# Split weights of the up stages at a place of their own in every group of 16 blocks (a two-layer decoder trunk on one core)

## The chip, the cores and the metric

The program runs on one core of a Trainium2 chip, in one launch. The metric is the time of one execution in microseconds (us) on the device. TensorE (PE) multiplies: a matmul loads up to 128 columns of weights (PEld in the profile) and then moves the columns of the other operand past them. VectorE (DVE), ScalarE (ACT) and GpSimd (POOL) do the elementwise work, and SyncE (SP) issues the large transfers. All of them work on a memory of 128 partitions (SBUF); the place of a tile is a byte address, the same in every partition.

## The reference

256 tokens of width 1024 pass two layers. Layer 0 has a mixer of two attention groups, layer 1 a latent attention; each is followed by the same channel mixer over 16384 single-neuron experts, and a norm ends the trunk. Of the channel mixer this matters here:

```python
def peer_ffn(h, w_q, sub_keys, u_tab, v_tab):
    ...
        q = (xc @ w_q).reshape(t, PEER_HEADS, 2, PEER_QDIM // 2)
        sc = jnp.einsum('thpc,hpnc->thpn', q, sub_keys).astype(jnp.float32)
        v_half, i_half = lax.top_k(sc, PEER_TOPK_HALF)
        ...
        top_s, pos = lax.top_k(cand, PEER_TOPK)
        expert = jnp.take_along_axis(cand_idx, pos, axis=-1)
        g = jax.nn.softmax(top_s, axis=-1)
        u = u_tab[expert]
        act = jax.nn.gelu(jnp.einsum('thkd,td->thk', u, xc).astype(jnp.float32), approximate=False)
        w = (g * act).astype(xc.dtype)
        return jnp.einsum('thk,thkd->td', w, v_tab[expert])
```

`u_tab` and `v_tab` are 16384 x 1024 in float32.

## The kernel before

The kernel gathers no experts. It multiplies the tokens with all of `u_tab` (the **up stage**), applies the gate, which is zero for experts that were not chosen, and multiplies with all of `v_tab` (the **down stage**). Both tables are cut into 128 blocks of 128 experts. A block of `u_tab` arrives as one `raw` tile of 128 x 1024, eight pieces of 128 x 128 side by side, one for each eighth of the model's width.

To keep float32's precision, every weight is split into two parts: `hi`, a copy by ACT into the type float32r (line 69), and `lo`, what is left, subtracted by DVE (line 70). The class `Weights` does this in halves of 512 columns. Its list `units` has an access pattern and a width for every `raw` tile in the order of use. `split` takes a `hi` tile from the pool `hip` and a `lo` tile from `lop`, with five buffers of 128 x 512 each, and runs four halves ahead of the use; `load` fetches `raw` two units ahead. Weights of all stages pass through this class.

In the up stage the split weights are the loaded operand, and the tokens' tiles `hi[c]` and `lo[c]` (128 x 256, eight of each, made once a layer) move past them. `split_prod` (line 814) multiplies one half: four pieces by three products, `hi` with `hi` (line 819), `hi` with the tokens' `lo` (line 820), and `lo` with `hi` (line 821). So a block has 24 matmuls of 128 x 128 weights and 256 moving columns into one tile `S`, and a layer has 3072. Between the halves `bg.pump` puts in pieces of background work: the routing on DVE, and from about block 33 on the gates, whose 512 small matmuls a layer stand on line 1011. In the down stage and in the projections the roles are exchanged: there the split weights move, 512, 352 or 200 columns at a time (lines 1099 to 1101 and 301 to 303).

Pools take their places one after the other: `cp` (tokens `x`, the identity matrix `ident` and other constants), `rawp`, `hip`, `lop`, `small`, then a tile `fill` of 192 bytes that nothing uses, and behind it the pools of the stage. As the program is built, `x`, `ident`, `raw`, all buffers of `hip` and `lop`, and the stages' tiles for the tokens' parts and the gates begin 160 bytes past a multiple of 512. The work tiles `rr` of the first mixer begin at a multiple of 512, and `ks` of the second one at 416 past one. The 200-column projection takes two 200-column pieces from one half, 800 bytes apart. A transpose (lines 288, 497 and 713) loads the tile that it turns and moves `ident` past it.

Of the kernel before, what the change touches and what calls it, by code (L numbers as in the profile page):

```python
# [10 lines left out]
F32R = mybir.dt.float32r  # L11
# [27 lines left out]
class Weights:  # L39
# [3 lines left out]
    def __init__(self, tc, nc, rawp, hip, lop, units, ahead=2, look=4):  # L43
        self.tc = tc
        self.nc, self.rawp, self.hip, self.lop = nc, rawp, hip, lop
        self.units, self.ahead, self.look = units, ahead, look
        self.raw, self.parts = [], {}
        self.halves = [(k, s) for k, (ap, w) in enumerate(units) for s in range(ap.shape[1] // w)]
        self.n_split = 0
        self.pos = 0  # L50

    def load(self, k):
        while len(self.raw) <= min(k, len(self.units) - 1):
            ap, w = self.units[len(self.raw)]
            t = self.rawp.tile([128, 1024], F32, name="raw")
            self.nc.sync.dma_start(t[:, :ap.shape[1]], ap)
            self.raw.append(t)

    def split(self, j):
        while self.n_split <= min(j, len(self.halves) - 1):  # L60
            k, s = self.halves[self.n_split]
            self.load(k + self.ahead)
            w = self.units[k][1]
            hi = self.hip.tile([128, 512], F32R, name="hi")
            self.tc_hp = self.tc.high_priority(offset=HP)
            self.tc_hp.__enter__()
            lo = self.lop.tile([128, 512], F32R, name="lo")
            src = self.raw[k][:, s * w:(s + 1) * w]
            self.nc.scalar.activation(hi[:, :w], src, AF.Copy)  # L69
            self.nc.vector.tensor_tensor(lo[:, :w], src, hi[:, :w].bitcast(F32), op=OP.subtract)  # L70
            self.tc_hp.__exit__(None, None, None)
            self.parts[self.n_split] = (hi, lo)
            self.n_split += 1
# [73 lines left out]
def body(tc, I, out):  # L147
    nc = tc.nc
    with ExitStack() as ctx:
# [9 lines left out]

        units = []  # L160

        def add(ap, w):
            for a in range(ap.shape[0]):
                units.append((ap[a], w))

        for k, v in PLAN0:
            if k == "P":
                add(I["w0s"] if v == "s" else I["w0"]["iq qa qk0 vb qk1".split().index(v)], 400 if v == "s" else 512)
            elif k == "O":
                add(I["w0o"][int(v):int(v) + 1], 512)  # L170
        add(I["pq"][0], 512)
        add(I["pu"][0], 512)
        add(I["pv"][0], 512)
        for k, v in PLAN1:
            if k == "P" and v[0] == "c":
# [4 lines left out]
            elif k == "O":  # L180
                add(I["w1o"][int(v):int(v) + 1], 512)
        add(I["pq"][1], 512)
        add(I["pu"][1], 512)
        add(I["pv"][1], 512)
        W = Weights(tc, nc, rawp, hip, lop, units)
        bg = Background(3)
# [995 lines left out]
```

## Time and profile before

| | us |
|---|---|
| median of 3 runs | 1887.8 (1887.28 to 1888.87) |
| profiled execution, whole | 1887.42 |
| its span, first to last instruction | 1885.6 |
| PE busy | 1863.1 (99%) |
| DVE busy | 1433.7 (76%) |
| ACT busy | 1248.0 (66%) |
| up stage of layer 0 / layer 1 | 403.64 / 403.65 |
| everything else | 1078.3 |

The page sums up one execution: what each engine did, the clock that PE was granted, and the chain of work that ended last. Matmuls overlap in the profile: one of 256 columns is shown with 0.28 us, although the next one starts earlier. What counts is how far apart they start, which the view in order of time shows.

### The profile page before, as it was taken

The numbers are of one execution on the slowest core, as the hardware profiler recorded it, in microseconds if no ns is written. First come the engines' busy times: TensorE is split into PE (matmuls) and PEld (weight loads), VectorE is DVE, ScalarE is ACT, GpSimd is POOL, SyncE is SP. The second block draws the span as 40 slices with busy tenths as digits, with TensorE's granted clock in tenths as the row PEclk, the third lists the DMA queues.
The fourth block names the chain that finished last, engine by engine and source line by source line (L and its number), as shares of the span: only waits on it lengthen the run. The fifth ranks groups of instructions, "written<-read, shape, count | busy, mean of one in ns | idle before, by whom it ended". The sixth has DMA issues, their size and how long they took to land.

```text
span 1885.6 us, 35589 instructions
## 1 busy us (share of the span) xinstructions
PE 1863.1 (99%) x12568; PEld 1687.9 (90%) x12568; DVE 1433.7 (76%) x3586; ACT 1248.0 (66%) x3060; POOL 15.0 (1%) x34
## 2 busy tenths in 40 slices
PE   9999999999999999999999999999999999999998
PEld 7779999999999888888888899999999988888886
DVE  7968998878897666666677699987788976666665
ACT  5656557888876555555577565578888765555554
POOL 0000000000000000000000000000000000000000
PEclk9999999999999999999999999999999999999999
DMA  6434555555455665555553345555555555665664
GB/s 201 124 112 146 185 180 174 167 161 166 158 160 176 192 196 193 192 197 192 184 167 122 124 148 189 183 166 163 161 164 162 168 178 191 193 197 191 193 197 147
DMA packets 90178, 323.33 MB, mean 171 GB/s; under 512 B 10512, under 2 KB 10896, under 8 KB 89744
## 3 DMA queue, kind: packets, MB, share of 16 engines
q1 hardware_dynamic: 88416, 318.18, 52.9%
q8 instruction: 99, 1.62, 0.4%
q0 software_dynamic: 288, 2.10, 0.3%
q10 hardware_dynamic: 1296, 0.78, 0.1%
q14 instruction: 79, 0.65, 0.1%
HBM read 319.97 MB, written 1.05 MB: 170 GB/s over the span
## 4 chain that ended last, share of the span: by engine, by line
PE 95%; DVE 3%; ACT 1%; issue 0%; DMA 0%; POOL 0%; DVEq 0%; POOLq 0%; ACTq 0%
PE S L819 15%; PE S L820 15%; PE S L821 15%; PE acc L1099 12%; PE acc L1101 12%; PE acc L1100 12%; PE scp L1011 3%; PE pj L301 2%; PE pj L303 2%; PE pj L302 2%; DVE lo L70 1%; PE bk L375 1%; PE scp L1048 1%; PE pj L439 1%; PE pj L440 1%; PE pj L441 1%
## 5 line engine op out<-in xcount | busy, mean ns | idle before, releaser
L69 ACT ACTIVATE hi<-raw 128x512 fp32r<-128x512 f32 (+2 forms) x1214 | 756.2, 628 | 567.2 <-PE S L820 191.0
L70 DVE TENSOR_TENSOR lo<-raw,hi 128x512 fp32r<-128x512 f32 (+2 forms) x1214 | 825.8, 685 | 370.8 <-ACT hi L69 362.4
L819 PE MATMUL S<-hi,hi 128*128 128x256 f32 x2048 | 591.0, 289 | 0.5 <-ACT A L1040 0.5
L820 PE MATMUL S<-lo,hi 128*128 128x256 f32 x2048 | 580.6, 284 | 0.0
L821 PE MATMUL S<-hi,lo 128*128 128x256 f32 x2048 | 580.1, 284 | 0.0
L819 PEld LDWEIGHTS S<-hi,hi 128*128 128x128 f32 x2048 | 393.4, 192 | 0.9 <-ACT A L1040 0.9
L820 PEld LDWEIGHTS S<-lo,hi 128*128 128x128 f32 x2048 | 393.8, 192 | 0.0
L821 PEld LDWEIGHTS S<-hi,lo 128*128 128x128 f32 x2048 | 393.0, 192 | 0.0
L1100 PE MATMUL acc<-lo,ohB 128*128 128x512 f32 x512 | 199.5, 390 | 0.0
L1100 PE MATMUL acc<-lo,ohA 128*128 128x512 f32 x512 | 199.5, 390 | 0.0
L1101 PE MATMUL acc<-hi,ohA 128*128 128x512 f32 x512 | 199.2, 390 | 0.0
L1101 PE MATMUL acc<-hi,ohB 128*128 128x512 f32 x512 | 198.5, 390 | 0.0
L1099 PE MATMUL acc<-hi,ohB 128*128 128x512 f32 x512 | 158.5, 390 | 0.0
L1099 PE MATMUL acc<-hi,ohA 128*128 128x512 f32 x512 | 158.2, 390 | 0.0
L976 ACT ACTIVATE ohB<-ohB,RA 128x128 bf16<-128x128 bf16 x256 | 117.2, 525 | 0.0
L1099 PEld LDWEIGHTS acc<-hi,ohA 128*128 128x128 f32 x512 | 96.2, 188 | 19.9
L1100 PEld LDWEIGHTS acc<-lo,ohA 128*128 128x128 f32 x512 | 96.2, 188 | 19.9
L1101 PEld LDWEIGHTS acc<-hi,ohB 128*128 128x128 f32 x512 | 96.2, 188 | 19.9
L1101 PEld LDWEIGHTS acc<-hi,ohA 128*128 128x128 f32 x512 | 96.2, 188 | 19.8
L1099 PEld LDWEIGHTS acc<-hi,ohB 128*128 128x128 f32 x512 | 96.2, 188 | 19.8
L1100 PEld LDWEIGHTS acc<-lo,ohB 128*128 128x128 f32 x512 | 96.1, 188 | 19.9
L1040 ACT ACTIVATE A<-S 128x256 f32<-128x256 f32 (+43 forms) x252 | 76.0, 302 | 13.3 <-PE S L821 13.2
(261 smaller groups left out, 2428.9 us busy)
## 6 DMA issues: line engine op xcount, KB each, us to landing
raw<-in_pu SPq DMA_DIRECT2D x256, 512.0 KB, 3.5
raw<-in_pv SPq DMA_DIRECT2D x256, 512.0 KB, 4.3
raw<-in_pq SPq DMA_DIRECT2D x32, 512.0 KB, 3.5
raw<-in_w SPq DMA_DIRECT2D x20, 512.0 KB, 3.9
raw<-in_uq SPq DMA_DIRECT2D x9, 512.0 KB, 4.1
raw<-in_w SPq DMA_DIRECT2D x12, 352.0 KB, 3.0
raw<-in_w0o SPq DMA_DIRECT2D x8, 512.0 KB, 3.6
raw<-in_w1o SPq DMA_DIRECT2D x8, 512.0 KB, 3.5
```

Source lines behind the costliest of these rows:

```text
L69: self.nc.scalar.activation(hi[:, :w], src, AF.Copy)
L70: self.nc.vector.tensor_tensor(lo[:, :w], src, hi[:, :w].bitcast(F32), op=OP.subtract)
L301: nc.tensor.matmul(ps[tb], hi[c][:, t], a, start=st, stop=False)
L819: nc.tensor.matmul(p, a, hi[c], start=first and i == 0, stop=False)
L820: nc.tensor.matmul(p, a, lo[c], start=False, stop=False)
L821: nc.tensor.matmul(p, b, hi[c], start=False, stop=last and i == 3)
L976: nc.scalar.activation(e[:, j // 2, :, j % 2], e[:, j // 2, :, j % 2], AF.Relu, bias=r[1], scale=r[2])
L1011: nc.tensor.matmul(p[:, i], E[:, 1, i // 2, :, i % 2], G[:, s, i // 2, :, i % 2], start=i + s == 0, stop=True, skip_group_check=True)
L1040: nc.scalar.activation(a[:, T:], p[:, T:], AF.Gelu)
L1099: nc.tensor.matmul(o, a[:, 0, t], w[0], start=b == 0, stop=False)
L1100: nc.tensor.matmul(o, a[:, 0, t], w[1], start=False, stop=False)
L1101: nc.tensor.matmul(o, a[:, 1, t], w[0], start=False, stop=b == NK - 1)
```

## The change

The tiles of `hip` and `lop` become 640 columns wide, and each split uses 512 of them, from an offset that the unit carries. The offset is zero everywhere but in the up stages. There it is 16 columns (64 bytes) times the number of the group of 16 blocks, 0 to 7, and 8 columns (32 bytes) more in layer 1. So layer 0 has the places 0, 64, ... 448 bytes and layer 1 has 32, 96, ... 480, on top of the buffer's own. A buffer of either pool grows from 2048 to 2560 bytes, so `lop` begins 2560 bytes later, and `small` and all tiles of the stages 5120 bytes later. On every engine the instructions stand in the same order as before, with the same waits.

```diff
-        self.halves = [(k, s) for k, (ap, w) in enumerate(units) for s in range(ap.shape[1] // w)]
+        self.halves = [(k, s) for k, (ap, w, o) in enumerate(units) for s in range(ap.shape[1] // w)]
...
-            w = self.units[k][1]
-            hi = self.hip.tile([128, 512], F32R, name="hi")
+            _, w, o = self.units[k]
+            hi = self.hip.tile([128, 640], F32R, name="hi")[:, o:o + 512]
...
-            lo = self.lop.tile([128, 512], F32R, name="lo")
+            lo = self.lop.tile([128, 640], F32R, name="lo")[:, o:o + 512]
...
-        def add(ap, w):
+        def add(ap, w, place=lambda a: 0):
             for a in range(ap.shape[0]):
-                units.append((ap[a], w))
+                units.append((ap[a], w, place(a)))
...
-        add(I["pu"][0], 512)
+        add(I["pu"][0], 512, lambda b: b // 16 * 16)
...
-        add(I["pu"][1], 512)
+        add(I["pu"][1], 512, lambda b: b // 16 * 16 + 8)
```

## Rows read from the trace of the kernel before

**Rows 1.** The page: busy time, granted clock in 40 slices, last chain.

```profile
span 1885.6 us, 35589 instructions
...
PE 1863.1 (99%) x12568; PEld 1687.9 (90%) x12568; DVE 1433.7 (76%) x3586; ACT 1248.0 (66%) x3060; POOL 15.0 (1%) x34
...
PEclk9999999999999999999999999999999999999999
...
PE 95%; DVE 3%; ACT 1%; issue 0%; DMA 0%; POOL 0%; DVEq 0%; POOLq 0%; ACTq 0%
```

**Rows 2.** Windows, up groups 1 and 8: length, engines' busy us (xcount), clock; both layers' sums.

```profile
191.92:238.52 46.60, 46.60 (x392) 46.60 (x391) 46.60 (x246) 27.01 (x51) 0.00 (x0) 1.00 0.59 189
...
543.68:595.56 51.88, 51.88 (x476) 51.41 (x474) 46.90 (x111) 39.88 (x119) 0.00 (x0) 1.00 0.52 163
sum 403.64, PE 403.41 PEld 400.39 DVE 350.80 ACT 304.68 POOL 0.00; mean PE 50.43 PEld 50.05 DVE 43.85 ACT 38.09 POOL 0.00
...
sum 403.65, PE 403.42 PEld 400.40 DVE 350.79 ACT 304.54 POOL 0.00; mean PE 50.43 PEld 50.05 DVE 43.85 ACT 38.07 POOL 0.00
```

**Rows 3.** PE in order of time (start us, us); then durations (ns, min/median/max).

```profile
205.04 0.28 PE L819 MATMUL S<-hi,hi 128*128 128x256 f32 x1
205.16 0.28 PE L820 MATMUL S<-lo,hi 128*128 128x256 f32 x1
205.28 0.28 PE L821 MATMUL S<-hi,lo 128*128 128x256 f32 x1
...
L819 PE MATMUL S<-hi,hi x2048: 278/284/385, 191.9 to 1527.8; 128*128 128x256 f32 x187
```

**Rows 4.** Order of time: eight matmuls of the gates.

```profile
344.57 0.64 PE L1011 MATMUL scp<-ohA,ohB 128*128 128x128 f16 x8
```

**Rows 5.** PE's waits: total us, times, longest.

```profile
PE S L819 <- ACT A L1040: 0.5, 2, 0.2
```

**Rows 6.** The page, groups of the split: count, busy us, mean ns, idle before.

```profile
L69 ACT ACTIVATE hi<-raw 128x512 fp32r<-128x512 f32 (+2 forms) x1214 | 756.2, 628 | 567.2 <-PE S L820 191.0
L70 DVE TENSOR_TENSOR lo<-raw,hi 128x512 fp32r<-128x512 f32 (+2 forms) x1214 | 825.8, 685 | 370.8 <-ACT hi L69 362.4
```

**Rows 7.** Order of time: PE in the down stage and in a 352-column projection.

```profile
609.64 0.39 PE L1100 MATMUL acc<-lo,ohA 128*128 128x512 f32 x1
...
610.55 0.62 PE L1099 MATMUL acc<-hi,ohA 128*128 128x512 f32 x2
...
958.63 0.33 PE L303 MATMUL pj<-hi,lo 128*128 128x352 f32 x1
958.79 0.32 PE L302 MATMUL pj<-lo,hi 128*128 128x352 f32 x1
```

**Rows 8.** Order of time: PE in the 200-column projection.

```profile
10.84 0.28 PE L302 MATMUL pj<-lo,hi 128*128 128x200 f32 x1
10.95 0.27 PE L301 MATMUL pj<-hi,hi 128*128 128x200 f32 x1
...
18.13 0.27 PE L301 MATMUL pj<-hi,hi 128*128 128x200 f32 x1
18.24 0.27 PE L302 MATMUL pj<-lo,hi 128*128 128x200 f32 x1
```

**Rows 9.** Order of time: transposes in a row, of three tiles; durations of one (ns).

```profile
35.02 0.60 PE L497 MATMUL bk<-ident,rr 128*128 128x128 f32 x4
...
135.77 0.71 PE L288 MATMUL acc<-ident,x 128*128 128x128 f32 x5
...
982.51 1.47 PE L713 MATMUL bk<-ident,ks 128*96 128x128 f32 x12
...
L713 PE MATMUL bk<-ident,ks x32: 271/273/313, 981.6 to 1022.7; 128*96 128x128 f32 x32
```

**Rows 10.** Durations on DVE (ns, min/median/max).

```profile
L334 DVE TENSOR_TENSOR rr<-rt,rt x8: 682/684/689, 30.6 to 89.0; 128x512 f32<-128x512 f32 x8
...
L463 DVE TENSOR_TENSOR x<-x,pj x8: 680/684/689, 131.8 to 1065.3; 128x512 f32<-128x512 f32 x8
```

More of the change, by code (lines that the diff above doesn't have):

```diff
@@ L53, in load @@
         while len(self.raw) <= min(k, len(self.units) - 1):
-            ap, w = self.units[len(self.raw)]
+            ap, w, _ = self.units[len(self.raw)]
             t = self.rawp.tile([128, 1024], F32, name="raw")
```

## Prediction

> **What bounds the kernel now.** I read the page first, then the two up stages in windows, then single matmuls in order of time. The page shows TensorE (PE) busy 99% of the span at the full granted clock in every slice, and the chain that ended last is PE for 95% of the span [rows 1]. The up stages are PE too: cut into their eight groups of 16 blocks, they take 403.64 us in layer 0 and 403.65 us in layer 1, PE is busy in 403.41 and 403.42 us of these, and the clock is 1.00 throughout [rows 2]. So the two stages are 807 of 1885.6 us, and whatever the change does must go through the rate of their 2 x 3072 matmuls (128 blocks, 24 each).
>
> That rate is even. In a clean stretch a matmul of 256 columns starts every 0.12 us [rows 3], and 3072 x 0.12 = 369 us. Most of the other 35 us of a stage are the 512 small matmuls of the gate work that stand between them from the third group on: eight in a row take 0.64 us with the last one's end, so at most 0.08 us each and 41 us together [rows 4]. That is also why the last group takes 51.88 us and the first 46.60 [rows 2]. The waits agree: before an up matmul PE is listed with 0.5 us of waiting, for ACT's work on an earlier block, and with none for a split [rows 5], while ScalarE (ACT) sat 191.0 us before its `hi` copies until PE had given a buffer back [rows 6]. The splits are early, PE is late.
>
> What is in the 0.12 us? In the down stage a matmul of 512 columns starts every 0.2275 us (0.91 us for four), and with 352 columns every 0.16 us [rows 7]. From 256 to 512 columns that is 0.107 us for 256 more, 0.42 ns a column; so 256 columns are 107 ns and 13 ns are left, and 352 columns give 147 + 13 = 160, as read. So every matmul pays about 13 ns beside its moving columns for its weights. The weights' load itself has a floor: with only 200 columns (84 + 13 = 97 ns by that sum) matmuls still start 110 ns apart [rows 8]. An up matmul therefore has 10 ns of room behind the load and none behind its moving columns.
>
> **The change part by part.** No instruction is added, removed or moved on any engine, and none waits for anything else; the tiles of the split weights grow from 2048 to 2560 bytes a partition, and the split of block b lies 64 x (b // 16) bytes into its tile, 32 more in layer 1. Everything else follows from places.
>
> (1) *TensorE reads the weights at other places.* Today weights, layer tiles, `x` and `ident` all begin 160 bytes past a multiple of 512; a matmul's weights are 512 bytes, the moving tile 1024, so weight loads and moving columns of an up stage always begin at the same place modulo 512. After the change they are apart by 0, 64, ... 448 bytes in layer 0 and 32, 96, ... 480 in layer 1: one group in 16 stays as it was, and 15 x 384 = 5760 matmuls are at a new distance. The trace of before has no up matmul at another distance, so the cost is bounded from both sides. Above: if all of the 110 ns load were to stand in the way instead of 13 ns, 97 ns x 5760 = 559 us. Below: if the 13 ns vanished, the load's floor still allows only 10 ns x 5760 = 58 us. Between these I take **zero**, by the nearest rows in which the distance does vary. The transposes load their tile and move `ident`. Those of `ks` load one head after the other from 416 on, 384 bytes apart, so 256, 128, 0 and 384 bytes from `ident` modulo 512: twelve of them in a row take 1.47 us, the last one 0.27, so 0.109 us each [rows 9]. Those of `rr`, which begins at a multiple of 512 (distance 352), run at (0.60 - 0.27) / 3 = 0.11 us, and those of `x`, at 160 like `ident`, at (0.71 - 0.27) / 4 = 0.11 us [rows 9]. In the 200-column projection a half holds two moving pieces, the second 800 bytes behind the first, so the load lies 0 or 224 from them: matmuls on a second piece (10.84 us) and on a first one (18.13) start 0.11 us apart alike [rows 8]. That is six of the change's sixteen distances (0, 128, 224, 256, 352, 384), at one rate to some ns. What these rows can't exclude: they are of matmuls with other columns, in which the load or the columns have some room. 1 ns of an up matmul is 5.8 us of the kernel.
>
> The Trainium skill, TensorE: Matmul & The Clock Gate, section The mechanism, says that a weight load runs beside a matmul in flight only where the two use different rows of the array. By that rule each nanosecond of a longer load would count from the first one, and the 10 ns of room would not be there; the trace speaks against it here, since a load with a floor of 110 ns and 107 ns of columns stand in one step of 120 [rows 3, 8]. The sum by the rule is still zero as long as the load itself is no longer.
>
> (2) *ACT and VectorE (DVE) write the splits at other places.* The `lo` subtraction takes 685 ns on average [rows 6]. The same operation on `x` at place 160 has a median of 684, and on `rr` at place 0 again 684, each within 5 ns of it [rows 10]. So zero again, bounded by that spread at 9 ns x 480 moved splits = 4.3 us of DVE, either way. It would be hidden: DVE is busy in 350.80 of 403.64 us and ACT in 304.68 [rows 2], PE waits for neither. The cover is thin in one place, the first group of a layer, where DVE is busy 46.60 of 46.60 us; there only layer 1's 32 splits are moved, at most 0.3 us.
>
> (3) *All that lies behind the two pools moves* by 2560 bytes (`lo`) and 5120 bytes (stage tiles), multiples of 512, so distances modulo 512 stay in every other stage. The ten split buffers are 2 KB apart and the 16 layer tiles 1 KB apart today, and the up matmuls on them have a median of 284 ns and a minimum of 278 [rows 3]; a shift of some KB shows nothing. Zero, and the other 1078 us of the span stay.
>
> The sum is 0 against the profiled execution's own 1887.42 us (span 1885.6 plus 1.8 around it), which is 0.4 us under the median of the runs shown, 1887.8. **Forecast: 1887.8 us, no change.** About 0.2%, or 3.8 us, is what a measurement of this kernel can tell from no change.
>
> **The rivals.** *Slower: today's common place is the good one.* If a weight load begun elsewhere than the moving columns gets in their way, the up matmul has nothing behind which to hide it: PE is on the path, and the columns have no room. For it: all stages with these 13 ns have everything at the same place modulo 512, so only the rows of (1) speak against it. It decides from 3.8 / 5.76 = 0.66 ns a matmul. At 1 ns it gives 1887.8 + 5.8 = 1893.6 us; if half of the new places cost a second step of 13 ns, 2880 x 13 = 37 us and 1925.
>
> *Faster: today's common place is the bad one.* Then the 13 ns are a clash of load and columns that begin at the same place, and other places win up to the load's floor: 10 ns in half of the new places is 29 us, 1859; in all of them 58 us, 1830. Against it: the sum of columns + 13 holds at 256, 352 and 512 columns to the nanosecond, which looks like a fixed price of changing weights and not like a clash along the columns; and transposes at the same and at other distances run alike [rows 7, 9].
>
> *Splits come late.* If `lo` took 10% longer (69 ns x 480 = 33 us of DVE), the idle 53 us of DVE in each stage take it, except in the full first group of layer 1: 32 x 69 ns = 2.2 us, 1890.0, which still counts as no change.
>
> **How the numbers follow.** No change 0.80 (the late splits 0.03 of it), slower 0.12, faster 0.08; the signs follow the cases one to one. The forecast's own range is 1884.0 to 1891.6. The slower rival is likelier at its small end, so the range reaches to 1893.5, which takes in a cost of just under 1 ns a matmul; below it ends at 1884.5. About 0.08 is left out above and 0.08 below.
>
> **What would show it.** Windows over the eight groups of each up stage are the test, since each group has its own place: the forecast wants the eight times of before in both layers again, from 46.6 to 51.9 us [rows 2], and steps of 0.12 us in any group. The slower rival shows some groups longer, by 0.38 us for each nanosecond (384 matmuls), with PE busy in them, and layer 0's first group as it was; the faster one shows them shorter. If the late splits are it, PE's waits for `hi` or `lo` appear in the first group of layer 1. A time that moves while all 16 groups stand would be (3) gone wrong: then down stages or mixers differ. A single group off by more than 2 us proves my zero wrong.

## The result and the profile after

The changed kernel takes 1877.47 us (median of 3 runs, 1877.02 to 1879.03) against 1887.8: a ratio of 0.9943 with an interval from 0.9926 to 0.9961. It is 10.3 us faster, where I had forecast no change.

The page of the changed kernel (busy time, clock, last chain, then the groups of the split) answers to [rows 1] and [rows 6]:

```profile
span 1875.6 us, 35589 instructions
...
PE 1853.4 (99%) x12568; PEld 1677.3 (89%) x12568; DVE 1432.4 (76%) x3586; ACT 1247.2 (66%) x3060; POOL 15.0 (1%) x34
...
PEclk9999999999999999999999999999999999999999
...
PE 93%; DVE 5%; ACT 1%; issue 1%; DMA 0%; POOL 0%; DVEq 0%; POOLq 0%; ACTq 0%
...
L70 DVE TENSOR_TENSOR lo<-raw,hi 128x512 fp32r<-128x512 f32 (+2 forms) x1214 | 825.1, 684 | 365.9 <-ACT hi L69 359.9
```

The span is 10.0 us shorter, PE is still the bound with 99%, at the same clock, and its busy time is 9.7 us less for the same 12568 matmuls. DVE's `lo` takes 684 ns on average, as before 685. So nothing waits less: the matmuls themselves are denser.

The windows over the eight groups of layer 0's up stage, then the sums of layer 0 and of layer 1, answer to [rows 2] (length, busy us of PE, PEld, DVE, ACT, POOL with counts, clock, share and rate of the DMAs):

```profile
191.90:238.49 46.59, 46.59 (x391) 46.59 (x390) 46.59 (x246) 26.98 (x51) 0.00 (x0) 1.00 0.59 189
238.49:283.94 45.45, 45.14 (x390) 44.93 (x388) 43.55 (x123) 27.96 (x54) 0.00 (x0) 1.00 0.57 184
283.94:333.53 49.59, 49.59 (x445) 49.28 (x444) 40.67 (x91) 38.45 (x106) 0.00 (x0) 1.00 0.54 173
333.53:384.73 51.20, 51.20 (x477) 50.68 (x474) 41.34 (x101) 42.50 (x132) 0.00 (x0) 1.00 0.52 165
384.73:436.52 51.79, 51.79 (x475) 51.32 (x473) 41.58 (x99) 42.69 (x131) 0.00 (x0) 1.00 0.48 157
436.52:487.00 50.48, 50.48 (x482) 49.99 (x481) 44.02 (x101) 43.36 (x136) 0.00 (x0) 1.00 0.54 177
487.00:539.00 52.00, 52.00 (x482) 51.47 (x481) 45.44 (x107) 42.63 (x130) 0.00 (x0) 1.00 0.50 164
539.00:590.14 51.14, 51.14 (x477) 50.65 (x474) 46.69 (x111) 39.81 (x119) 0.00 (x0) 1.00 0.52 166
...
sum 398.24, PE 397.93 PEld 394.90 DVE 349.88 ACT 304.37 POOL 0.00; mean PE 49.74 PEld 49.36 DVE 43.74 ACT 38.05 POOL 0.00
...
sum 398.97, PE 398.69 PEld 395.57 DVE 350.19 ACT 303.93 POOL 0.00; mean PE 49.84 PEld 49.45 DVE 43.77 ACT 37.99 POOL 0.00
```

The two up stages are 5.4 and 4.7 us shorter (403.64 to 398.24, 403.65 to 398.97). That is the whole gain. Groups 2 to 7 of layer 0 in the kernel before (groups 1 and 8 stand in [rows 2]):

```profile
238.52:285.39 46.87, 46.64 (x389) 46.44 (x388) 44.05 (x123) 27.93 (x54) 0.00 (x0) 1.00 0.58 180
285.39:335.33 49.94, 49.94 (x445) 49.64 (x444) 40.65 (x90) 38.47 (x106) 0.00 (x0) 1.00 0.55 171
335.33:387.27 51.94, 51.94 (x477) 51.43 (x474) 41.33 (x102) 42.52 (x132) 0.00 (x0) 1.00 0.51 161
387.27:439.07 51.80, 51.80 (x475) 51.33 (x473) 41.56 (x99) 42.67 (x131) 0.00 (x0) 1.00 0.51 158
439.07:491.44 52.37, 52.37 (x482) 51.82 (x481) 44.22 (x102) 43.52 (x136) 0.00 (x0) 1.00 0.54 170
491.44:543.68 52.24, 52.24 (x482) 51.73 (x481) 45.47 (x107) 42.68 (x130) 0.00 (x0) 1.00 0.51 163
```

The first and the fifth group stand where they were: their places are 0 and 256 bytes. The second and the sixth, at 64 and 320 bytes, are 1.4 and 1.9 us shorter, the third and the seventh (128 and 384) 0.35 and 0.24, the fourth and the eighth (192 and 448) 0.74 both. So a group's time follows its place, and it repeats after 256 bytes, to some tenths of a us.

Single matmuls in order of time, in the second group of layer 0 (64 bytes), to be read beside [rows 3] (start us, shown length us):

```profile
240.02 0.28 PE L820 MATMUL S<-lo,hi 128*128 128x256 f32 x1
240.14 0.28 PE L821 MATMUL S<-hi,lo 128*128 128x256 f32 x1
240.26 0.28 PE L819 MATMUL S<-hi,hi 128*128 128x256 f32 x1
240.38 0.28 PE L820 MATMUL S<-lo,hi 128*128 128x256 f32 x1
240.49 0.28 PE L821 MATMUL S<-hi,lo 128*128 128x256 f32 x1
...
255.94 0.28 PE L819 MATMUL S<-hi,hi 128*128 128x256 f32 x1
256.06 0.28 PE L820 MATMUL S<-lo,hi 128*128 128x256 f32 x1
256.17 0.28 PE L821 MATMUL S<-hi,lo 128*128 128x256 f32 x1
256.28 0.28 PE L819 MATMUL S<-hi,hi 128*128 128x256 f32 x1
256.39 0.28 PE L820 MATMUL S<-lo,hi 128*128 128x256 f32 x1
```

Early in the group four steps take 0.47 us, 0.1175 each; 16 us later, with the same places, four take 0.45, 0.1125. Before, it was 0.12 everywhere. The view rounds to 10 ns; the trace has start times to 1 ns. By these the steps of this group are 117.8 ns in some stretches and 113.3 ns in others, and the change from one to the other comes where work of another kind has stood between the matmuls.

### The profile page after: what moved, and what is told of

It is laid out like the page before. It is cut to its first block, busy times and chain, and to the rows that moved or that the text cites. A ratio compares the mean times of both kernels' runs of the same rounds, so it can differ in the third digit from the quotient of the medians.

```text
span 1875.6 us, 35589 instructions
## 1 busy us (share of the span) xinstructions
PE 1853.4 (99%) x12568; PEld 1677.3 (89%) x12568; DVE 1432.4 (76%) x3586; ACT 1247.2 (66%) x3060; POOL 15.0 (1%) x34
## 4 chain that ended last, share of the span: by engine, by line
PE 93%; DVE 5%; ACT 1%; issue 1%; DMA 0%; POOL 0%; DVEq 0%; POOLq 0%; ACTq 0%
PE S L819 14%; PE S L820 14%; PE S L821 14%; PE acc L1099 12%; PE acc L1101 12%; PE acc L1100 12%; PE scp L1011 3%; PE pj L301 2%; PE pj L303 2%; PE pj L302 2%; DVE lo L70 2%; PE bk L375 1%; PE scp L1048 1%; PE pj L439 1%; PE pj L440 1%
## 5 line engine op out<-in xcount | busy, mean ns | idle before, releaser
L820 PE MATMUL S<-lo,hi 128*128 128x256 f32 x2048 | 574.7, 281 | 0.0
L819 PEld LDWEIGHTS S<-hi,hi 128*128 128x128 f32 x2048 | 386.7, 189 | 1.0 <-ACT A L1040 1.0
L820 PEld LDWEIGHTS S<-lo,hi 128*128 128x128 f32 x2048 | 386.9, 189 | 0.0
L821 PEld LDWEIGHTS S<-hi,lo 128*128 128x128 f32 x2048 | 385.5, 188 | 0.0
L978 ACT ACTIVATE ohB<-iota,RA 128x128 bf16<-128x128 f32 x256 | 84.1, 435 | 0.0
```

Source lines behind the costliest of these rows:

```text
L819: nc.tensor.matmul(p, a, hi[c], start=first and i == 0, stop=False)
L820: nc.tensor.matmul(p, a, lo[c], start=False, stop=False)
L821: nc.tensor.matmul(p, b, hi[c], start=False, stop=last and i == 3)
L978: nc.scalar.activation(e[:, j // 2, :, j % 2], iota, AF.Square, bias=r[0], scale=-1.0)
```

## The experiments

In what follows a *distance* is the place that a load reads minus the place of the moving columns, modulo 256 bytes; a *step* is the mean time from one matmul's start to the next one's, where no other work and no wait stands between, taken from start times to 1 ns. The edits are shown against the changed kernel, unless said otherwise.

**Theory D**: the distance sets the step. **Rivals**: the shift of all later tiles by some KB did it; the variation does it and not the place; the weights' own place counts (and so ACT's and DVE's writing of them); what else runs in a group does it.

**The shift alone** (`wide0`):

```diff
-        add(I["pu"][0], 512, lambda b: b // 16 * 16)
+        add(I["pu"][0], 512)
...
-        add(I["pu"][1], 512, lambda b: b // 16 * 16 + 8)
+        add(I["pu"][1], 512)
```

> The tiles stay 640 columns wide and all tiles behind the two pools stay 2560 or 5120 bytes further on, but every offset is zero. Theory D (the distance between the place that the weight load reads and the place of the moving columns, modulo 256 bytes, sets the up matmul's step): all distances are zero again, steps of 120 ns in all 16 groups, 1887.8 us within 2. Rival S (the shift of the stage tiles by some KB brought the gain): 1877.5 us, and the groups are as short as in the changed kernel.

Measured: 1889.22 us beside 1888.14 on the same chip, ratio 1.0002 (0.9992 to 1.0012). All 16 groups step at 119.9 to 120.0 ns. The shift is worth nothing; part (3) of the prediction stands.

**One place for all** (`up64`):

```diff
-        add(I["pu"][0], 512, lambda b: b // 16 * 16)
+        add(I["pu"][0], 512, lambda b: 16)
...
-        add(I["pu"][1], 512, lambda b: b // 16 * 16 + 8)
+        add(I["pu"][1], 512, lambda b: 16)
```

> All blocks of both layers use the offset of 64 bytes. Theory D: in the changed kernel the groups at 64 and 320 bytes ran at mean steps of 115.95 and 114.62 ns against 119.9, so all 6144 matmuls win 4.0 to 5.3 ns: 24 to 33 us, 1855 to 1864 us. Rival V (what helps is that the place varies from group to group, not which place it is): a constant place brings nothing, 1887.8 us. Rival P (these two groups are short for what else runs in them, at their point of the stage): the other groups stay at 118 to 120 ns and the time stays near 1877.

Measured: 1860.83 us, ratio 0.9855 (0.9839 to 0.9872). So it is the place and not its variation, and it works in every group: 113.5 to 115.5 ns in groups 3 to 8 of layer 0, and 117.8 and 116.7 in the first two, which stay longer at the 117.8 ns rate.

**The moving side instead** (`fill128`, from the kernel before):

```diff
-        ctx.enter_context(tc.tile_pool(name="fill", bufs=1)).tile([128, 48], F32, name="fill")
+        ctx.enter_context(tc.tile_pool(name="fill", bufs=1)).tile([128, 32], F32, name="fill")
```

> The kernel before, with the unused tile of 192 bytes cut to 128: the split weights stay where they were, and all stage tiles lie 64 bytes lower. Up stages: load minus moving is again 64 bytes, now by the moving side's place. Theory D: up steps of 114.6 to 116 ns as with the offset of 64, 24 to 33 us less; in the down stages and projections the loaded tile is the one that moved, load minus moving is 192, and if their 13 ns have the same cause they win some 2 ns each (as the up groups at 192 did, 117.8 against 119.9), another 7 us: 1848 to 1857 us. Rival W (the weights' own place counts, not the distance): up steps stay at 120 ns, 1887.8 us. If only the down stage stays at 227 ns, its 13 ns have another cause: 1855 to 1864.

Measured: 1865.88 us, ratio 0.9878 (0.9862 to 0.9895). Windows over groups 4 to 6 of layer 0's up stage (columns as in [rows 2]), first with the weights 64 bytes further, then with the tokens' tiles 64 bytes lower:

```profile
333.19:383.26 50.07, 50.07 (x477) 49.61 (x474) 41.29 (x101) 42.45 (x132) 0.00 (x0) 1.00 0.50 169
383.26:432.72 49.46, 49.46 (x475) 49.07 (x473) 41.33 (x98) 42.71 (x131) 0.00 (x0) 1.00 0.50 166
432.72:483.18 50.46, 50.46 (x483) 49.97 (x481) 44.26 (x102) 43.36 (x136) 0.00 (x0) 1.00 0.54 177
```

```profile
334.41:384.48 50.07, 50.07 (x477) 49.61 (x474) 41.30 (x101) 42.50 (x132) 0.00 (x0) 1.00 0.51 168
384.48:433.94 49.46, 49.46 (x475) 49.07 (x473) 41.31 (x98) 42.77 (x131) 0.00 (x0) 1.00 0.50 166
433.94:484.39 50.45, 50.45 (x482) 49.96 (x481) 44.24 (x102) 43.42 (x136) 0.00 (x0) 1.00 0.55 177
```

These groups agree to 0.01 us, and the seventh and eighth do too, although ACT and DVE write the weights at different places in the two. The first three do not: 45.76, 45.74 and 47.79 us with the weights moved, 46.09, 45.99 and 47.99 with the tokens' tiles moved, at steps of 117.8, 116.7 and 114.0 ns against 115.6, 115.9 and 114.6. They lie between the same two rates, 117.8 and 113.3 ns, but not equally long at each. So the distance counts, between the two reads of PE; it sets which rates can occur, and not alone which of them does. But the total is 5 us worse than that of `up64`, where I expected it better: the down stage, now at distance 192, steps at 228.9 ns and not at 226.7 as before, 2.2 x 3072 = 7 us more. That expectation, that the down stage gains by the same distances, was wrong.

**A finer scan of the up stage** (`fine`):

```diff
-        add(I["pu"][0], 512, lambda b: b // 16 * 16)
+        add(I["pu"][0], 512, lambda b: (4, 12, 20, 28, 36, 44, 52, 60)[b // 16])
...
-        add(I["pu"][1], 512, lambda b: b // 16 * 16 + 8)
+        add(I["pu"][1], 512, lambda b: (13, 14, 15, 17, 18, 19, 22, 24)[b // 16])
```

> Offsets by group of 16 blocks: layer 0 16, 48, 80, 112, 144, 176, 208, 240 bytes; layer 1 52, 56, 60, 68, 72, 76, 88, 96 bytes. Theory D with a smooth dependence: steps lie between those of the neighbours in the changed kernel (120.0 at 0, 118.3 at 32, 115.3 at 64, 118 at 96, 119 at 128, 119.8 at 160, 117.8 at 192, 116.9 at 224), and layer 1 runs at 114 to 117.5 ns with its least near 64; total about 1866 to 1873 us. If the dependence has steps of some block size, places within the same block give the same time to 0.2 ns. If 64 is a lone point, all of layer 1 is at 117 ns or more.

Measured: 1878.24 us in one run, above the 1866 to 1873 that a smooth dependence wanted. The steps, in ns: 118.3, 118.0, 118.7, 120.0, 119.8, 118.1, 116.7, 119.4 in layer 0, and 119.8 (52 bytes), 117.8 (56), 119.6 (60), 118.4 (68), 118.4 (72), 114.1 (76), 113.5 (88), 117.9 (96) in layer 1. The dependence does not look smooth: neighbours 4 bytes apart differ by up to 4 ns. But each place stands here for one group, and at 64 bytes the groups of `up64` differ among themselves by as much (113.5 to 117.8), so a single difference here may be one of rates and not of places. Nor is 64 a lone point. 0 and 112 are the worst places seen (120.0 both).

**Two good places, and a scan of the down stage** (`scan2`; the numbers count columns of 4 bytes):

```diff
-        add(I["pu"][0], 512, lambda b: b // 16 * 16)
-        add(I["pv"][0], 512)
+        add(I["pu"][0], 512, lambda b: 22)
+        add(I["pv"][0], 512, lambda b: (8, 16, 24, 32, 40, 48, 56, 4)[b // 16])
...
-        add(I["pu"][1], 512, lambda b: b // 16 * 16 + 8)
-        add(I["pv"][1], 512)
+        add(I["pu"][1], 512, lambda b: 19)
+        add(I["pv"][1], 512, lambda b: (12, 20, 28, 36, 44, 52, 60, 64)[b // 16])
```

> Up stages: one place each, 88 bytes in layer 0 and 76 in layer 1 (the two single groups of the fine scan that ran at 113.5 and 114.1 ns). Down stages: the split weights, which move there, lie 32, 64, 96, 128, 160, 192, 224, 16 bytes further in layer 0's groups and 48, 80, 112, 144, 176, 208, 240, 256 in layer 1's, so load minus moving is minus that, modulo 256. Theory D: layer 0's up groups all run at 113.3 to 114.5 ns, layer 1's at 114 to 115, some 38 us less together; the down steps differ by group: 226.7 again at 256, 228.9 at 64 (distance 192, as with the stage tiles moved by 64), and somewhere below 226.7 if the 13 ns there are collisions of the same kind, down to 220. Rival L (88 and 76 are chance states of their groups): up groups spread between 113 and 120. Rival F (the 13 ns of the down stage are the fixed price of changing weights): no down group under 226.6.

Measured: 1875.59 us in one run. 76 bytes holds, 113.5 to 114.8 ns in all groups; 88 does not, 113.5 to 116.7, so the 113.5 of that one group was one of two rates and not fixed by the place. Windows over 192 matmuls of the down stage (length, PE busy, clock, DMA share and rate), of the kernel before and of this one (32, 64 and 96 bytes):

```profile
639.11:682.63 43.52, 43.52 (x193) 1.00 0.60 193
682.63:726.15 43.52, 43.52 (x193) 1.00 0.60 195
```

```profile
584.14:628.94 44.80, 44.80 (x195) 1.00 0.58 188
628.94:672.88 43.94, 43.94 (x193) 1.00 0.57 192
672.88:717.69 44.81, 44.81 (x193) 1.00 0.57 188
```

All of the tried distances from 16 to 240 step at 228.9 to 234.6 ns, and only 0 (the group at 256 bytes) gives 226.7. As rival F wanted, no group is under 226.6, but the price is not fixed either: it changes with the distance. Distance 192 gives 228.9 here, by the split weights' place, and gave 228.9 in `fill128`, by the other tile's, so in the down stage too it is the distance that counts. The down stage is at its best where the up stage is at its worst. It took back 16 us of the up stage's 29.

**Only the `hi` parts moved** (`lo_at0`, with 76 bytes for the up units):

```diff
-            lo = self.lop.tile([128, 640], F32R, name="lo")[:, o:o + 512]
+            lo = self.lop.tile([128, 640], F32R, name="lo")[:, :512]
```

> In the up stages only the `hi` parts lie at 76 bytes, the `lo` parts at 0. It tells which load stands in the way of which moving columns. A matmul's step here is from its start to the next one's. Theory D with the load of the next matmul beside the columns of this one: the `lo` weights (for line 821) are loaded while line 820 moves, so line 820's step is the long one, 118 to 120 ns, and lines 819 and 821 stay at 113 to 115. With the matmul's own load: line 821's step is the long one. If a step depends on the whole history (one clash shifts the next), all three lines lie between. Total between 1855 and 1875 us.

Measured: 1874.3 us in one run. Lines 819, 820 and 821 step at 118.2, 116.6 and 117.9 ns in the mean, so neither simple form of the theory holds. In some stretches the steps repeat as 120, 113, 114 (one long step, that of line 821, for the one load in three at distance 0), in others all are 117 to 118, and in others again line 819 has 120 and the other two 116 to 117. The last alternative fits: a step depends on what went before. Which load meets which columns stays open.

**All matmuls of this form at 76 bytes** (`all76`):

```diff
-        add(I["pq"][0], 512)
-        add(I["pu"][0], 512, lambda b: b // 16 * 16)
+        add(I["pq"][0], 512, lambda b: 19)
+        add(I["pu"][0], 512, lambda b: 19)
...
-        add(I["pq"][1], 512)
-        add(I["pu"][1], 512, lambda b: b // 16 * 16 + 8)
+        add(I["pq"][1], 512, lambda b: 19)
+        add(I["pu"][1], 512, lambda b: 19)
```

> 76 bytes for the split weights of both up stages and of both query projections (the 768 matmuls of the same form with the tokens' raw tiles), zero for all others, so the down stages keep distance 0, the best of their sixteen. Theory D: up steps 113.5 to 114.8 ns in all 16 groups (as layer 1 of the scan before), 6144 x 5.9 = 36 us; query steps from 119.5 to some 114, 768 x 5.5 = 4 us; down steps 226.67; 1888 - 40 = 1848 us. If the query projection has another pattern, 1852. If the shorter up stage is then held by VectorE, PE shows waits for splits and the time stays above 1856.

Measured: 1856.91 us, ratio 0.9835 (0.9818 to 0.9851). The steps came as expected, 113.5 to 114.8 ns, but 8 us of the sum did not. Windows over the first two groups of layer 0 (columns as in [rows 2]); behind them the chain that ended last in the first 22 us of these, by line; what PE's loads (PEld) waited for in both groups; and two instructions of ACT in order of time:

```profile
191.69:237.89 46.20, 45.72 (x391) 44.70 (x390) 46.20 (x242) 25.65 (x51) 0.00 (x0) 1.00 0.56 185
237.89:284.06 46.17, 44.39 (x390) 44.12 (x389) 45.25 (x134) 27.82 (x55) 0.00 (x0) 1.00 0.59 191
```

```profile
by line: DVE lo L70 31.3%; DVE A L855 21.2%; DVE A L859 19.7%; DVE A L852 16.3%; issue 9.1%; DVE A L878 3.6%; PE S L821 1.8%
...
PEld S L819 <- ACT A L1040: 2.3, 2, 2.0
PEld S L821 <- DVE lo L70: 1.2, 4, 0.4
...
251.89 1.28 ACT L1040 ACT_TABLE_LOAD   x1
253.19 0.38 ACT L1040 ACTIVATE A<-S 128x256 f32<-128x256 f32 x1
```

DVE is busy in 46.20 of 46.20 us of the first group, and the group is hardly shorter than before (46.60) although its clean steps are 6 ns shorter. Its first half hangs on DVE: `lo` and the routing (lines 852 to 878) make up 92% of the chain, and PE's loads wait for `lo`. There the routing on DVE has become the bound, the cover that I had called thin. The second group is another case. PE is idle for 1.8 us, nearly all in one wait, and that wait ends with ACT: its line 1040 reads a buffer `S` out, and stands behind an `ACT_TABLE_LOAD` of 1.28 us. The same instruction stood there in the kernel before, when PE waited 0.2 us for it. Together the first two groups of both layers are 2.9 us shorter than before, where their clean steps alone would give some 9: that is 6 to 7 of the 8 us.

**The same without the query projections** (`up76`): the two lines of `pq` are left as they were.

> 76 bytes for the split weights of both up stages alone; query projections and down stages as before, at distance 0. The kernel with the query projections at 76 too had up steps of 113.5 to 114.8 ns and 1856.9 us, with PE held up in the first group of blocks of each layer, where VectorE is full. Theory Q (the faster query projection gains nothing, since VectorE's routing work behind it is what the first up groups wait for): the up stages begin some 3 us later in each layer, and wait less in the first group; 1855 to 1860 us. If the query projection's 4 us were a true gain: 1861.

Measured: 1858.76 us, ratio 0.9839 (0.9823 to 0.9855), not to be told from `all76`. In layer 0 the query projection takes 55.7 us and not 54.0, the up stage 388.5 and not 390.2: what the projection gains is given back behind it, as expected. In layer 1 it is 56.3 and not 54.1, and 388.7 and not 389.6, so there only a part is given back.

**Off the multiples of 16 bytes in the down stage** (`scan3`, with 76 bytes for the up units):

```diff
-        add(I["pv"][0], 512)
+        add(I["pv"][0], 512, lambda b: (1, 2, 3, 5, 6, 7, 9, 10)[b // 16])
...
-        add(I["pv"][1], 512)
+        add(I["pv"][1], 512, lambda b: (61, 62, 63, 45, 42, 19, 22, 25)[b // 16])
```

> Up stages at 76 bytes. In the down stages the moving split weights lie 4, 8, 12, 20, 24, 28, 36, 40 bytes further in layer 0's groups and 244, 248, 252, 180, 168, 76, 88, 100 in layer 1's. Theory D, if in the down stage too some places off the multiples of 16 bytes reach one 16-cycle step less (as 76 and 88 did in the up stage, 113.3 where 0 gives 120.0): some groups at 220 ns. If distance 0 is the best place there: all 16 groups between 227 and 235 ns. Total 1865 to 1880 us.

Measured: 1877.09 us in one run. Windows over the groups at 20, 24 and 28 bytes:

```profile
716.13:762.21 46.08, 46.08 (x194) 1.00 0.55 183
762.21:807.02 44.81, 44.81 (x194) 1.00 0.58 187
807.02:850.54 43.52, 43.52 (x193) 1.00 0.60 193
```

Offsets of 28 and 252 bytes give the step of distance 0 (226.7 ns); all others lie between 228.3 and 240.0, beyond the 235 that I expected at most. No place that was tried beats 0. Here 4 bytes do change the step, from 240.0 at 20 to 233.4 at 24 and 226.7 at 28, while all 16 down groups of `fill128`, at one distance, agree to 0.1 ns.

## Why the prediction was wrong

**What bounds the kernel.** Right: the time went through the rate of the up matmuls and through nothing else, and the test that I named, the 16 groups, showed it at once.

**Step (1), zero for the loads at other places: the step that failed.** It should have been -10 us: 5760 moved matmuls at 1.7 ns each. The bound below (10 ns) holds: the shortest steady step seen is 113.3 ns, 6.7 less. What went wrong is the choice of rows. I took six distances at one rate as the nearest evidence, with the remark that these matmuls have room in the load or in the columns, and then gave the remark no weight. In the 200-column projection the load's 110 ns stand against 84 ns of columns, 97 with the 13 ns. The transposes move other data: 128 of their columns take 0.109 us [rows 9], as long as 256 of an up matmul, 107 ns. What hides the distance there, if anything does, was not tried, and room alone can't be it: in the down stage the load has the most room (110 ns beside 213 of columns), and that step moves the most, by 13 ns. Both views show a floor and not the term that I wanted to bound. The up matmuls themselves (256 columns, load and columns both near 110 ns) all had distance 0, so the rows that I took held no evidence for zero.

The reading was also too coarse for the term. Modulo 256 bytes the six distances are four, 0, 96, 128 and 224, and the changed kernel's up groups at these stepped at 120.0, 118, 119 and 116.9 ns. So 1 to 3 ns had to be seen, in rows that are rounded to 10 ns, and 10 ns of 5760 matmuls are 58 us. By start times to 1 ns, the 200-column matmuls of [rows 8] and those around them start, within a run of them, 108 to 117 ns apart: "0.11 us apart alike" could not bound a term that decides from 0.66 ns.

**The argument against the faster rival failed with it.** "Columns + 13 ns at 256, 352 and 512 columns" looked like a fixed price of changing weights. It is not fixed: at other distances the up stage pays 6 to 13 ns beside its columns (113.3 to 120.0) and the down stage 13 to 27 (226.7 to 240.0). In the kernel before, all these stages load 128 columns at the same distance, so my three rows could not tell a fixed price from one that hangs on the distance. Why it comes to 13 ns at distance 0 with 256 and with 512 columns alike, no run shows.

**The rivals.** The faster one was right in its main point: the common place is a bad one for the up stage. It is not bad only because both begin at the same place, since 112 and 160 bytes gave 120.0 and 119.8 ns. Its size was too large, 29 us for half of the places, since most new places gain 1 to 3 ns and not 10; its full case of 58 is not reached by any place tried (27 to 32 us in the best kernels). The slower one is true of the down stage, where the common place is the good one; the change did not touch it. The third rival, late splits, cost nothing here. Splits came late in `all76`, not since `lo` took longer (685 ns there too) but since PE was faster.

**Steps (2) and (3)** hold. DVE's `lo` took 684 ns after 685, and the shift alone gave 1.0002.

**The cited rule.** The sentence cited from the Trainium skill, that a load runs beside a matmul only where their rows of the array differ, finds no support: a load with a floor of 110 ns and 107 ns of columns fit into steps of 113.3. (The same section also lets loads into a background weight buffer run ahead; by the cited sentence alone they could not.) The same page of the Trainium skill (TensorE: Matmul & The Clock Gate, section Step-by-step: what each phase is for) says that moving columns and weight loads have two independent read ports. In time they are not independent here: the step moves by 6.7 ns in the up stage and by 13 in the down stage with nothing changed but the distance of the two reads.

**What stays open.** What the two reads share (the period of 256 bytes and, in the down stage, the sensitivity to 4 bytes are all that the runs tell), why one place has two steady rates, 117.8 and 113.3 ns, and which pair of load and columns clashes. That the distance of the two reads is the cause is shown; how it acts is not.

## What to carry to other kernels

Where every matmul loads its own weights, put the tiles that are loaded and those that move at a chosen distance, scan it in one run by giving each stretch its own place, and judge each stage for itself: the place that is worst for one shape can be the best for another. A trace in which all places are equal says nothing about places; rows of another shape don't stand in for it, and rows rounded to 10 ns can't bound a term of 1 ns. When the bound gets faster, look at what it then waits for, stretch by stretch: here DVE in the first group of a layer and ACT in the second took back 6 to 7 us of 40.

## What the runs showed of the hardware

- The step of a matmul with 128 loaded and 256 moving columns (float32r) lay between 113.3 and 120.0 ns in steady stretches, with 512 moving columns between 226.7 and 240.0, by the distance of the two tiles in the memory, modulo 256 bytes.
- The same distance gives the same steps whichever of the two tiles is moved: 50.07, 49.46 and 50.46 us a group against 50.07, 49.46 and 50.45 in the up stage (the first three groups of a layer differ by up to 0.4 us), and 228.9 ns both ways in the down stage.
- At 64 bytes the steps settle at 117.8 or at 113.3 ns and, in all but one stretch of the two kernels with this distance throughout, stay there until other work comes between.
- The best kernels put all up weights at 76 bytes and leave the down stage at 0: 1856.9 and 1858.8 us, ratios 0.9835 (0.9818 to 0.9851) and 0.9839, ahead of both kernels of this study.
